# Squares of branch B by whole tiles, key norm rows loaded a head ahead, index scores paced by the heads of C and B

## The chip, the cores and the metric

The kernel runs on one core of one Trainium2 chip. The metric is device time in microseconds (us) of one execution, lower is better. The core has five engines with queues of their own: PE (matmuls; PEld is its weight load), DVE (VectorE), ACT (ScalarE), POOL (GpSimd, used here almost only to issue DMAs) and SP (issues DMAs). Each runs its own instructions in order and waits for others by semaphores.

## The reference

One decoder layer over 512 tokens of width 2048, in float32. `h = rms_norm(x)` is projected once, and the columns feed three branches, a SiLU gate for each, and three merge gates:

```python
# A: sparse attention: index scores pick the 128 best keys of each query
dots  = einsum('bthd,bsd->bths', q_idx, k_idx)           # 16 index heads of 64
score = einsum('bths,bth->bts', relu(dots), w_idx) * IDX_SCALE
_, sel = top_k(where(causal, score, -inf), topk)         # then GQA over sel, 8 heads, bias by distance
# B: latent attention, 8 heads; 192 = 128 plain + 64 rotary
qb = rms_norm((rms_norm(bcq)  @ w_b_uq ).reshape(bsz, seq, 8, 192))
kv =          (rms_norm(bckv) @ w_b_ukv).reshape(bsz, seq, 8, 256)     # 128 key + 128 value
kb = rms_norm(concat([kv[..., :128], k_pe]))             # rotary part shared by the heads
o_b = causal_softmax(rope(qb) @ rope(kb) * 192**-0.5) @ kv[..., 128:]
# C: cross-attention into 256 memory tokens, 4 heads of 256
u = stack([o_a * silu(az), o_b * silu(bz), o_c * silu(cz)])
merged = sum_n sigmoid(gates[n]) * (u[n] @ w_branch[n])
out = x + merged @ w_out
```

The norms of B's queries and keys need, for each token and head, a sum of squares over 128 plain columns, and over 64 rotary columns.

## The kernel before

**Main stream and threads.** `stream` on PE walks a list of weight chunks; each is cut into jobs of 256 weight rows, and a plain job has 24 matmuls of 512 columns. Weights arrive by SP (`wraw`, 512 KB), ACT rounds them to `whi`, DVE subtracts to get the rest `wlo`, and three matmuls (high by high, high by low, low by high) stand for one in float32. Jobs are prepared three ahead (`LOOK = 3`). The order of chunks is: memory keys and values, projections, merge gates (by Strassen products), a z chunk (SiLU gate) of C, `uq0` to `uq2` (B's queries from the latent; `uq2` holds the rotary parts), `ukv0` to `ukv3` (B's keys and values), the other z chunks, then four `w_branch` chunks each for C, B and A (the operand `u` is branch output times gate), and `w_out`. Results collect in PSUM: `pg` and `pn` for the main stream, `pm` for everything else.

All attention work is written as generators ("threads"): `c_thread` and `c_part` (C), `b_thread` and three `b_part` (B; one prepares head after head, the parts do logits, softmax and values for query tiles 0 and 1, 2, 3), `idx_thread` (index scores for eight pairs of heads into `mask1` to `mask3`, then top-k on DVE by 16 rounds of MAX and MATCH_REPLACE a tile), `a_bias_thread` and `a_thread` (A's bias and heads, after B has closed), `u_thread` (loads branch output and gate into `stage`, multiplies, splits into `u`).

**What sets the order.** The program is written once, by a planner: it books a modelled cost for each instruction on its engine, and after each group of three matmuls of the main stream it steps those threads whose inputs the model shows as ready. A `yield` of a list waits in the model for these tiles or for a free `pm` bank; a `yield` of a string waits for a flag set by another thread. These waits only decide where an instruction stands in its engine's queue; on the chip, semaphores for data and buffers are all that is left of them. `defer` puts a piece of work behind one of the next groups of matmuls.

**What the change touches.** `to_dram` evacuates a chunk of B two token tiles at a time into `stage` (one half by ACT, one by DVE), issues the store, and defers the squares: for `uq0`, `uq1` and `ukv*` one ACT square of 128x128 for each head and token tile into `junk` with an accumulated sum in `b_ss`; for `uq2` one whole square of `stage` into another `stage`, then one DVE sum into `r_ss`. `b_thread` makes the norms `rs_b` from `b_ss` and `r_ss`, stores those of the keys as rows in DRAM (`sp_rows`), and for each head loads the four rows broadcast over all partitions as `b_rk` (one buffer): after the three parts of the head before have set the flags `B0 scaled`, `B1 scaled` and `B2 scaled` in `softmax`. `rotate` turns the rotary query part `b_rp` with three scratch tiles `ro_a`, `ro_b`, `ro_c`. The pool `lpool` of the latents (`lraw`, `cqT`, `ckT`) is closed when the second z chunk of C begins on PE; `bpool` opens after that.

Of the kernel before, what the change touches and what calls it, by code (L numbers as in the profile page):

```python
# [10 lines left out]
F32 = mybir.dt.float32  # L11
# [4 lines left out]
OP = mybir.AluOpType  # L16
# [274 lines left out]
class Kern:  # L291
# [638 lines left out]
    def to_dram(self, key, nb, cols, scale=None, sums=(), groups=None):  # L930


        nc = self.nc
        dt = self.spill_tile(key, nb, cols)
        box = {}

        def evac(b, p):
            if b % 2 == 0:
                box["st"] = self.stage()
            st = box["st"]  # L940
            src, dst = p[:, :cols], st[:, b % 2, :cols]
# [12 lines left out]
            def squares():  # L954
                for c0, c1, d in sums:
                    junk = self.wp.tile([P, 512], BF, name="junk", tag="junk")
                    nc.scalar.activation(junk[:, :c1 - c0], st[:, b % 2, c0:c1], AF.Square, accum_out=d(b))
                if b == nb - 1:
                    self.flags.add(key + " sums")
            if sums:  # L960
                self.defer(squares, b == nb - 1)
            if groups and b % 2:
                sq = []

                def whole():
                    sq.append(self.stage())
                    nc.scalar.activation(sq[0], st, AF.Square)

                def total():
                    nc.vector.tensor_reduce(groups[:, b - 1:b + 1], sq[0].rearrange("p t (h c) -> p t h c", h=groups.shape[2]),  # L970
                                            axis=AX.X, op=OP.add)
                    if b == nb - 1:
                        self.flags.add(key + " sums")
                self.defer(whole, False, 2)
                self.defer(total, b == nb - 1)
        return evac
# [72 lines left out]
        tt(dst[:, :, 32:], a, b, op=OP.add)  # L1049


    def softmax(self, pool, blocks, scale, tag, act, bank, masks=None, flag=None):


        nc = self.nc
        n = len(blocks)
        st = pool.tile([P, 4, n], F32, name=tag + "st", tag=tag + "st", bufs=2)
        if masks:
            for i, ((pr, ps), (mk, rk)) in enumerate(zip(blocks, masks)):
                nc.vector.tensor_tensor(pr, ps, rk, op=OP.mult)  # L1060
                nc.vector.tensor_tensor_reduce(pr, pr, mk, 1.0, -3.4e38, OP.add, OP.max, st[:, 0, i:i + 1])
            self.pm.release(bank)
            self.flags.add(flag)
            nc.vector.scalar_tensor_tensor(st[:, 1], st[:, 0], -1.0, scale, op0=OP.mult, op1=OP.mult)
        else:
            for i, (_, ps) in enumerate(blocks):
                nc.vector.tensor_reduce(st[:, 0, i:i + 1], ps, axis=AX.X, op=OP.max, negate=True)
            nc.vector.tensor_tensor(st[:, 1], st[:, 0], scale, op=OP.mult)
        yield [st]
        for i, (pr, ps) in enumerate(blocks):  # L1070
            nc.scalar.activation(pr, pr if masks else ps, AF.Exp, bias=st[:, 1, i:i + 1], scale=scale[:, i:i + 1],
                                 accum_out=st[:, 2, i:i + 1])
        if not masks:
            self.pm.release(bank)
        yield [st]
        nc.vector.reciprocal(st[:, 3], st[:, 2])
        for i, (pr, _) in enumerate(blocks):
            if act:
                if not i:
                    yield [st]  # L1080
                nc.scalar.activation(pr, pr, AF.Copy, scale=st[:, 3, i:i + 1])
            else:
                nc.vector.tensor_scalar(pr, pr, st[:, 3, i:i + 1], None, op0=OP.mult)
# [130 lines left out]
    def b_thread(self):  # L1214
# [5 lines left out]
        with self.slots("bpool", side="right") as pool:  # L1220
# [13 lines left out]
                return rp  # L1234

            def load_scale(h):
                rk = pool.tile([P, T], F32, name="b_rk", tag="b_rk")
                row = rows[8 * h + 4:8 * h + 8]
                nc.gpsimd.dma_start(rk, bass.AP(tensor=row.tensor, offset=row.offset, ap=[[0, P], [1, T]]))
                return rk  # L1240
# [7 lines left out]
            def rotate(rp):  # L1248

                x = rp.rearrange("p t (a d) -> p t a d", a=2)  # L1250
                x1, x2 = x[:, :, :, :32], x[:, :, :, 32:]
                a, b, c = [pool.tile([P, NT, 2, 32], F32, name="ro_" + y, tag="ro_" + y) for y in "abc"]
                sin, cos = [bc(y, [P, NT, 2, 32], 2) for y in (self.sin, self.cos)]
                gain = self.g_bqr.unsqueeze(1).unsqueeze(1).to_broadcast([P, NT, 2, 64])
                tt = nc.vector.tensor_tensor
# [30 lines left out]
            pt = ring.bank([P, 512])  # L1286
            nc.tensor.transpose(pt[:64, :P], rs_b.rearrange("p a b -> p (a b)"), self.ident)
            yield [pt]
            stage = pool.tile([P, T], F32, name="b_rk", tag="b_rk")
            nc.scalar.activation(stage[:64, :P], pt[:64, :P], AF.Copy)  # L1290
            nc.gpsimd.dma_start(rows, stage[:64, :P])
            ring.release(pt)
# [11 lines left out]
            for h in range(8):  # L1304
# [21 lines left out]
                if h % 2 == 0:  # L1326
# [8 lines left out]
                    ring.release(pt)  # L1335
                    if h < 6:
                        rp = load_rope(h + 2)
                if h:
                    for x in range(3):
                        yield "B%d scaled %d" % (x, h - 1)  # L1340
                    rk = load_scale(h)
                self.b_now = (pool, rs, qh, ql, kh, kl, qs[h % 2], rh, rl, rk)
                self.flags.add("b%d" % h)
                if h:
                    yield "B2 %d" % (h - 1)
                vh = pool.tile([P, NT, P], F32R, name="b_vh", tag="b_vh")
                vl = pool.tile([P, NT, P], F32R, name="b_vl", tag="b_vl")
                yield from self.split_in_turn(vh, vl, kv[:, :, P:])
# [11 lines left out]
    def b_part(self, x):  # L1360
# [6 lines left out]
        for h in range(8):  # L1367
# [10 lines left out]
            for t in tiles:  # L1378
# [3 lines left out]
                for i, (a, b) in enumerate(((qh, kh), (qh, kl), (ql, kh), (qs, rh), (qs, rl))):  # L1382
# [3 lines left out]
            self.flags.add("B%d logits %d" % (x, h))  # L1386
            yield [pg, rk]
            yield from self.softmax(pool, blocks, rs[:, tiles[0]:tiles[-1] + 1], "b%d_" % x, True, pg,
                                    [(self.mwide[:, T - (t + 1) * P:], rk[:, :(t + 1) * P]) for t in tiles],
                                    "B%d scaled %d" % (x, h))  # L1390
            yield [pr, ring]
            pt = ring.bank([P, n, P])
            for b in range(n):
# [40 lines left out]
    def idx_thread(self, apre, kpool):  # L1434
# [4 lines left out]
        with self.slots("ipool", line=512) as pool:  # L1439
# [42 lines left out]
                        nc.vector.scalar_tensor_tensor(sc[t], x, iw[:, t, h:h + 1], sc[t], op0=OP.mult, op1=OP.add)  # L1482

            for hp in range(8):
                yield [q]
                s0 = pool.tile([P, 512], F32R, name="i_s0", tag="i_s0")
                s1 = pool.tile([P, 512], F32R, name="i_s1", tag="i_s1")
# [745 lines left out]
    def build(self):  # L2233
# [42 lines left out]
        def close_gates():  # L2276
# [7 lines left out]
            self.ckT = [self.lp.tile([P, 2, T], F32R, name="ckT%d" % i) for i in range(2)]  # L2284
            self.flags.add("gates")

        def close_h():
            yield "z end"
            yield "B closed"
            hpool2.close()  # L2290
            self.bp = bpool.enter_context(self.slots("bp", side="right"))
            self.flags.add("bp")
# [30 lines left out]
        def one(x, b):  # L2323
            return x[:, b:b + 1]
# [36 lines left out]
        pre(close_gates)  # L2361
        wu = A["w_uq"]
        for c in range(3):
            sums = [(j * P, j * P + P, lambda b, h=4 * c + j: one(self.b_ss[:, h], b)) for j in range(4 if c < 2 else 0)]
            self.chunk(wu[:, c * 512:(c + 1) * 512], 4, 512,
                       lambda k: (self.cqT[0][:, k], self.cqT[1][:, k]), "tm", 4,
                       self.to_dram("uq%d" % c, 4, 512, sums=sums, groups=None if sums else self.r_ss), "bcqT")
        wk = A["w_b_ukv"][0]
        for c in range(4):
            sums = [(j * 256, j * 256 + P, lambda b, h=2 * c + j: one(self.b_ss[:, h], 4 + b)) for j in range(2)]  # L2370
            self.chunk(wk[:, c * 512:(c + 1) * 512], 2, 512,
                       lambda k: (self.ckT[0][:, k], self.ckT[1][:, k]), "tm", 4,
                       self.to_dram("ukv%d" % c, 4, 512, sums=sums), "bckvT")
        for key in "ABC":
            for c in range(2):
                self.spill_tile("o%s%d" % (key, c), 4, 512)
        for n, c in ((2, 1), (0, 0), (0, 1), (1, 0), (1, 1)):
            z_chunk(n, c)
            if n == 2:
                self.chunks[-1]["start"] = "kpe"  # L2380
                pre(lambda: (lpool.close(), self.flags.add("latents done")))
        self.chunks[-1]["post"] = lambda: self.flags.add("z end")
        for i in range(2):
            self.spill_tile("m%d" % i, NT, D)
# [7 lines left out]
        def mem_load(eng, a, b):  # L2392
# [4 lines left out]
        w = None  # L2397
        self.first_loads = [w, m(0, 2), m(2, 4), w, m(4, 6), w, m(6, 8), w, m(8, 10), w, m(10, 12), w, m(12, 16), w]
        self.run(self.stream, [
            self.mem_thread(sp, memh, meml), self.x_loads(), self.x_thread(sp), self.mem_stats(sp), self.rotary_tables(), self.latent_thread(), self.u_thread(), self.kpe_thread(), self.c_thread(), self.c_part(0), self.c_part(1), self.b_part(0), self.b_part(1), self.b_part(2), self.b_thread(), self.a_thread(0), self.a_thread(1), self.a_bias_thread(apre, kpool), self.idx_thread(apre, kpool), self.h_ops_thread(), self.t_thread(), close_h()])  # L2400
        tpool.close()
        bpool.close()
        hpool.close()
# [35 lines left out]
```

## Time and profile before

| | |
|---|---|
| median of 3 runs | 1823.47 us (1823.46 to 1825.14) |
| profiled execution: its own time, its span | 1823.97 us, 1822.2 us |
| busy PE, PEld, DVE, ACT, POOL | 1810.0, 1512.8, 1371.7, 972.5, 193.5 us |
| DVE and ACT, 960 to 1040 us (chunks `uq`, `ukv` and around) | 48.0 and 63.3 us of 80 |
| DVE, 1160 to 1320 us (B's heads, top-k) | 148.0 us of 160 |
| top-k rounds on DVE | 1163.7 to 1339.8 us |
| first and last DVE operation on `b_pr` (B's logits) | 1088.9, 1297.6 us |
| last store of A's output (`sp_oA`) | issued at 1553.9 us |

The page's share of busy PE is no measure of waiting, since a matmul's record runs from its start until its result is out, and records overlap: here they start 0.227 us apart and last 0.39 us. What PE lost is seen where two starts stand further apart than the first of them takes in the stream.

### The profile page before, as it was taken

How to read it: one execution, taken by the hardware profiler on the slowest of the kernel's cores; microseconds unless marked ns; L12 is line 12 of the kernel's file. 1: busy time of each engine (PE TensorE's matmuls, PEld its weight loads, DVE VectorE, ACT ScalarE, POOL GpSimd, SP SyncE). 2: the span in 40 equal slices, each digit the busy share in tenths (PEclk: the TensorE clock that was granted, in tenths of full speed). 3: DMA queues.
4: the chain of work that ended last, by engine and by line, in shares of the span. 5: the costliest groups of instructions: out<-in, count | busy, mean ns of one | idle time of the engine just before them, and what ended most of it. 6: DMA issues, size and time to landing. Idle time of an engine off the chain costs nothing.

```text
span 1822.2 us, 24643 instructions
## 1 busy us (share of the span) xinstructions
PE 1810.0 (99%) x9009; PEld 1512.8 (83%) x9009; DVE 1371.7 (75%) x2098; ACT 972.5 (53%) x1740; POOL 193.5 (11%) x286
## 2 busy tenths in 40 slices
PE   9999999999999999999999999999999999899999
PEld 7888888888888888888888888888888888688887
DVE  6888787787777777778775677899986777566755
ACT  7644544554444444444458756545477875244442
POOL 0000101001010100000112121311011111110000
PEclk9999999999999999999999999999999999999999
DMA  9846597787676966756645544444664754746784
GB/s 379 293 161 196 188 331 199 199 215 201 186 291 217 264 189 193 208 162 200 208 158 204 190 152 137 139 155 116 213 238 158 248 162 163 277 162 197 269 268 144
DMA packets 155994, 374.84 MB, mean 206 GB/s; under 512 B 18656, under 2 KB 24192, under 8 KB 154848
## 3 DMA queue, kind: packets, MB, share of 16 engines
q1 hardware_dynamic: 116752, 236.79, 40.8%
q0 software_dynamic: 38976, 136.34, 23.3%
q8 instruction: 71, 1.16, 0.3%
q14 instruction: 51, 0.42, 0.1%
q10 hardware_dynamic: 144, 0.13, 0.0%
HBM read 314.69 MB, written 92.08 MB: 223 GB/s over the span
## 4 chain that ended last, share of the span: by engine, by line
PE 97%; DVE 1%; DMA 1%; ACT 0%; issue 0%; SPq 0%; DVEq 0%
PE pg L157 60%; PE pn L157 27%; PE pm L157 9%; DMA wraw<-w_in 1%; DMA wraw<-w_mem 0%; DVE wlo L157 0%; ACT a_st L157 0%; DVE yg L157 0%; DVE stage L157 0%; SPq L157 0%; DVE T L157 0%; ACT whi L157 0%; DVE bm L157 0%; DVE u L157 0%; DVE mask L157 0%
## 5 line engine op out<-in xcount | busy, mean ns | idle before, releaser
L157 DVE TENSOR_TENSOR wlo<-wraw,whi 128x1024 fp32r<-128x1024 f32 (+2 forms) x267 | 321.6, 1206 | 148.6 <-ACT whi L157 147.2
L157 ACT ACTIVATE whi<-wraw 128x1024 fp32r<-128x1024 f32 (+2 forms) x267 | 278.3, 1044 | 287.9 <-PE pg L157 155.5
L157 PE MATMUL pg<-whi,u 128*128 128x512 f32 x640 | 215.6, 398 | 0.5 <-DVE yg L157 0.5
L157 PE MATMUL pg<-hh,whi 128*128 128x512 f32 x448 | 179.9, 401 | 0.0
L157 PE MATMUL pg<-hh,wlo 128*128 128x512 f32 x448 | 175.3, 391 | 0.0
L157 PE MATMUL pg<-hl,whi 128*128 128x512 f32 x448 | 174.9, 390 | 0.0
L157 ACT ACTIVATE whi<-sraw 128x1024 fp32r<-128x1024 f32 (+1 forms) x99 | 103.7, 1049 | 127.2 <-DVE sraw L157 54.2
L157 DVE TENSOR_TENSOR wlo<-sraw,whi 128x1024 fp32r<-128x1024 f32 (+1 forms) x99 | 119.9, 1213 | 52.1 <-ACT whi L157 51.2
L157 PE MATMUL pg<-whi,hS 128*128 128x512 f32 (+1 forms) x480 | 156.8, 388 | 0.0
L157 PE MATMUL pn<-whi,hS 128*128 128x512 f32 (+1 forms) x480 | 156.1, 386 | 0.0
L157 PEld LDWEIGHTS pg<-whi,u 128*128 128x128 f32 x640 | 120.2, 188 | 23.9 <-DVE yg L157 0.9
L157 PE MATMUL pg<-wlo,u 128*128 128x512 f32 x320 | 124.8, 390 | 0.0
L157 PE MATMUL pg<-wlo,hh 128*128 128x512 f32 (+1 forms) x320 | 123.9, 387 | 0.0
L157 PE MATMUL pn<-wlo,hh 128*128 128x512 f32 (+1 forms) x320 | 123.8, 387 | 0.0
L157 PE MATMUL pg<-whi,hl 128*128 128x512 f32 (+1 forms) x320 | 123.8, 387 | 0.0
L157 PE MATMUL pn<-whi,hl 128*128 128x512 f32 (+1 forms) x320 | 123.8, 387 | 0.0
L157 PE MATMUL pn<-whi,hh 128*128 128x512 f32 (+1 forms) x320 | 123.8, 387 | 0.0
L157 PE MATMUL pg<-whi,hh 128*128 128x512 f32 (+1 forms) x320 | 123.8, 387 | 0.0
L157 ACT ACTIVATE whi<-T 128x1024 fp32r<-128x1024 f32 (+1 forms) x80 | 83.9, 1049 | 68.7 <-PE pn L157 26.0
L157 DVE TENSOR_TENSOR wlo<-T,whi 128x1024 fp32r<-128x1024 f32 (+1 forms) x80 | 96.7, 1209 | 30.4 <-ACT whi L157 30.2
L157 PEld LDWEIGHTS pg<-whi,hS 128*128 128x128 f32 x480 | 90.1, 188 | 18.0
L157 PEld LDWEIGHTS pn<-whi,hS 128*128 128x128 f32 x480 | 90.1, 188 | 17.3
(459 smaller groups left out, 3977.2 us busy)
## 6 DMA issues: line engine op xcount, KB each, us to landing
wraw<-w_in SPq DMA_DIRECT2D x146, 512.0 KB, 4.2
sraw<-w_in SPq DMA_DIRECT2D x90, 512.0 KB, 4.2
wT<-w_out POOLq DMA_DIRECT2D x24, 1024.0 KB, 20.8
wraw<-w_branch SPq DMA_DIRECT2D x48, 512.0 KB, 4.5
yg<-sp_g POOLq DMA_DIRECT2D x24, 512.0 KB, 6.0
wraw<-wT SPq DMA_DIRECT2D x20, 512.0 KB, 3.9
mraw<-w_mem SPq DMA_DIRECT2D x17, 512.0 KB, 8.4
wT<-wT POOLq DMA_DIRECT2D x8, 1024.0 KB, 13.0
```

What stands on the lines that cost most here:

```text
L157: return f(*a, **k)
```

## The change

1. **Squares.** For all `uq` and `ukv` chunks ACT squares both token tiles in one instruction, into a tile of the shape and the single buffer of `lraw`: 1024 columns a partition for `uq0` and `uq1` (four heads) and `uq2` (eight rotary parts), 512 for `ukv*` (only the key halves of two heads). DVE then sums by heads into `b_ss` or `r_ss`. The 64 small squares go.
2. **Latents.** Since `lraw` now serves the squares, the `uq` chunks wait for the second latent too (`"bckvT"`), and `lpool` is closed by a thread of its own, `close_latents`, after `kpe`, `uq2 sums` and `ukv3 sums`.
3. **Key norm rows.** `b_rk` has two buffers; the load for head h+1 stands after head h-1's last output instead of the load for head h after head h-1's last scaling. The flags `scaled` go.
4. **Rotary scratch.** `rotate` takes one `stage` buffer in place of `ro_a`, `ro_b`, `ro_c`.
5. **Pace.** Before each pair of index heads `idx_thread` waits for a flag: pair 0 for C's head 1, pair 1 for C's head 3, pair 2 for the end of C, pairs 4 to 7 for B's heads 1 to 4.

```diff
@@ to_dram
+                n, w, dst_of = groups
                 def whole():
-                    sq.append(self.stage())
-                    nc.scalar.activation(sq[0], st, AF.Square)
+                    y = self.lp.tile([P, NT, 256], F32, name="lraw", tag="lraw")...[:, :2 * n * w]...(t=2, h=n)
+                    sq.append(y)
+                    nc.scalar.activation(y, st[:, :, :cols]...(h=n)[:, :, :, :w], AF.Square)
                 def total():
-                    nc.vector.tensor_reduce(groups[:, b - 1:b + 1], sq[0]..., axis=AX.X, op=OP.add)
+                    nc.vector.tensor_reduce(dst_of(b - 1), sq[0], axis=AX.X, op=OP.add)
@@ b_thread
-                rk = pool.tile([P, T], F32, name="b_rk", tag="b_rk")
+                rk = pool.tile([P, T], F32, name="b_rk", tag="b_rk", bufs=2)
-                a, b, c = [pool.tile([P, NT, 2, 32], F32, name="ro_" + y, tag="ro_" + y) for y in "abc"]
+                room = self.stage().rearrange("p t c -> p (t c)")
+                a, b, c = [room[:, 256 * i:256 * i + 256]... for i in range(3)]
-                if h:
-                    for x in range(3):
-                        yield "B%d scaled %d" % (x, h - 1)
-                    rk = load_scale(h)
                 self.flags.add("b%d" % h)
                 if h:
                     yield "B2 %d" % (h - 1)
+                if h < 7:
+                    rk = load_scale(h + 1)
@@ idx_thread
             for hp in range(8):
+                pace = {0: "c1", 1: "c3", 2: "C"}.get(hp) or hp > 3 and "b%d" % (hp - 3)
+                if pace:
+                    yield pace
@@ build
+        def close_latents():
+            for x in ("kpe", "uq2 sums", "ukv3 sums"):
+                yield x
+            lpool.close()
+            self.flags.add("latents done")
-                       self.to_dram("uq%d" % c, 4, 512, sums=sums, groups=None if sums else self.r_ss), "bcqT")
+                       self.to_dram("uq%d" % c, 4, 512, groups=groups), "bckvT")
-                       self.to_dram("ukv%d" % c, 4, 512, sums=sums), "bckvT")
+                       self.to_dram("ukv%d" % c, 4, 512, groups=groups), "bckvT")
-                pre(lambda: (lpool.close(), self.flags.add("latents done")))
```

PE executes the same 9009 matmuls in both programs, by kind and count. Since the planner writes the order anew, what stands between the first z chunk of C and the start of branch A is in another order.

On ACT, at the evacuation of `uq0`, `junk,b_ss<-stage` is the four small squares of one token tile; its neighbours are index scores (`i_r`, `i_s`) and C's heads (`c_...`). Before:

```order
L157 ACTIVATE stage<-pg 128x512
L157 ACTIVATE junk,b_ss<-stage 128x128 x4
L157 ACTIVATE i_r<-pm_7809 128x512
L157 ACTIVATE i_s_7851<-i_q 64x512
L157 ACTIVATE i_s_7852<-i_q 64x512
L157 ACTIVATE whi<-wraw 128x1024
```

Now, at the first pair of token tiles of `uq0`:

```order
L157 ACTIVATE stage<-pg 128x512
L157 ACTIVATE lraw<-stage 128x1024
L157 ACTIVATE c_qh<-pm_7784,cols 128x512
L157 ACTIVATE c_pr<-pm_7789 128x512
L157 ACTIVATE c_pr<-pm_7802 128x512
L157 ACTIVATE i_r<-pm_7815 128x512
L157 ACTIVATE whi<-wraw 128x1024
```

Eight small squares of a pair of token tiles became one, and C's heads stand further ahead against the weights, with fewer index scores between them.

On SP, at the end of the `w_branch` chunks, `sp_oB` and `sp_oA` are the outputs of B and A, `sp_s` their gates; a `w_branch` load is one job of PE (- before, + now):

```order
 L157 DMA stage<-sp_oB_207 128x1024
-L157 DMA wraw<-w_branch 128x2x512 x2
+L157 DMA wraw<-w_branch 128x2x512 x3
 L157 DMA stage<-sp_s_211 128x1024
-L157 DMA wraw<-w_branch 128x2x512 x14
+L157 DMA wraw<-w_branch 128x2x512 x8
 L157 DMA stage<-sp_oA_204 128x1024
 L157 DMA stage<-sp_s_211 128x1024
 L157 DMA stage<-sp_oA_204 128x1024
-L157 DMA wraw<-w_branch 128x2x512
+L157 DMA wraw<-w_branch 128x2x512 x4
```

The first loads of A's output moved ahead by six jobs against the weights: the first stands behind 31 of the 48 `w_branch` loads instead of 37.

On DVE, at the end of branch B, `yg<-yg,pg` evacuates a bank of the last `w_branch` chunks, `yg<-ym,yg` adds the branches, and `stage<-stage` and `u<-stage,u` make the operand of branch A. Before, the first `u` of A stands behind the evacuation of B's last chunk, `a_pl` being the last splits of A's heads:

```order
L157 TENSOR_TENSOR a_pl<-pm_14390,a_ph 128x512
L157 TENSOR_TENSOR wlo<-wraw,whi 128x1024
L157 SCALAR_TENSOR_TENSOR yg<-yg,pg 128x512
L157 TENSOR_TENSOR wlo<-wraw,whi 128x1024
L157 SCALAR_TENSOR_TENSOR yg<-yg,pg 128x512 x3
L157 TENSOR_TENSOR yg<-ym,yg 128x512 x4
L157 SCALAR_TENSOR_TENSOR stage<-stage 128x1024
L157 TENSOR_TENSOR u<-stage,u 128x1024
```

Now it stands behind the evacuation of B's last chunk but one, with `stage<-stage` still ahead of that:

```order
L157 TENSOR_TENSOR a_pl<-pm_14079,a_ph 128x512
L157 TENSOR_TENSOR yg<-ym,yg 128x512
L157 TENSOR_TENSOR wlo<-wraw,whi 128x1024 x2
L157 SCALAR_TENSOR_TENSOR stage<-stage 128x1024
L157 SCALAR_TENSOR_TENSOR yg<-yg,pg 128x512
L157 TENSOR_TENSOR wlo<-wraw,whi 128x1024
L157 SCALAR_TENSOR_TENSOR yg<-yg,pg 128x512 x3
L157 TENSOR_TENSOR yg<-ym,yg 128x512 x2
L157 TENSOR_TENSOR wlo<-wraw,whi 128x1024
L157 TENSOR_TENSOR yg<-ym,yg 128x512 x2
L157 TENSOR_TENSOR u<-stage,u 128x1024
```

The operand of branch A moved ahead of the four evacuations of B's last chunk. On PE, 42 matmuls of branch B stand between the last matmul of A's heads and the first of branch A before the change, and 171 with it.

More of the change, by code (lines that the diff above doesn't have):

```diff
@@ L963, in evac @@
                 sq = []
+                n, w, dst_of = groups
                 def whole():
-                    sq.append(self.stage())
-                    nc.scalar.activation(sq[0], st, AF.Square)
+                    y = self.lp.tile([P, NT, 256], F32, name="lraw", tag="lraw").rearrange("p t c -> p (t c)")[:, :2 * n * w].rearrange("p (t h c) -> p t h c", t=2, h=n)
+                    sq.append(y)
+                    nc.scalar.activation(y, st[:, :, :cols].rearrange("p t (h c) -> p t h c", h=n)[:, :, :, :w], AF.Square)
                 def total():
-                    nc.vector.tensor_reduce(groups[:, b - 1:b + 1], sq[0].rearrange("p t (h c) -> p t h c", h=groups.shape[2]),
-                                            axis=AX.X, op=OP.add)
+                    nc.vector.tensor_reduce(dst_of(b - 1), sq[0], axis=AX.X, op=OP.add)
                     if b == nb - 1:
@@ L1049, in rotate, with softmax @@
         tt(dst[:, :, 32:], a, b, op=OP.add)
-    def softmax(self, pool, blocks, scale, tag, act, bank, masks=None, flag=None):
+    def softmax(self, pool, blocks, scale, tag, act, bank, masks=None):
         nc = self.nc
@@ L1062, in softmax @@
             self.pm.release(bank)
-            self.flags.add(flag)
             nc.vector.scalar_tensor_tensor(st[:, 1], st[:, 0], -1.0, scale, op0=OP.mult, op1=OP.mult)
@@ L1251, in rotate @@
                 x1, x2 = x[:, :, :, :32], x[:, :, :, 32:]
-                a, b, c = [pool.tile([P, NT, 2, 32], F32, name="ro_" + y, tag="ro_" + y) for y in "abc"]
+                room = self.stage().rearrange("p t c -> p (t c)")
+                a, b, c = [room[:, 256 * i:256 * i + 256].rearrange("p (t a d) -> p t a d", t=NT, a=2) for i in range(3)]
                 sin, cos = [bc(y, [P, NT, 2, 32], 2) for y in (self.sin, self.cos)]
@@ L1288, in b_thread @@
             yield [pt]
-            stage = pool.tile([P, T], F32, name="b_rk", tag="b_rk")
+            stage = pool.tile([P, T], F32, name="b_rk", tag="b_rk", bufs=2)
             nc.scalar.activation(stage[:64, :P], pt[:64, :P], AF.Copy)
@@ L1388, in b_part @@
             yield from self.softmax(pool, blocks, rs[:, tiles[0]:tiles[-1] + 1], "b%d_" % x, True, pg,
-                                    [(self.mwide[:, T - (t + 1) * P:], rk[:, :(t + 1) * P]) for t in tiles],
-                                    "B%d scaled %d" % (x, h))
+                                    [(self.mwide[:, T - (t + 1) * P:], rk[:, :(t + 1) * P]) for t in tiles])
             yield [pr, ring]
@@ L2363, in build @@
         for c in range(3):
-            sums = [(j * P, j * P + P, lambda b, h=4 * c + j: one(self.b_ss[:, h], b)) for j in range(4 if c < 2 else 0)]
+            groups = (4, P, lambda b, c=c: self.b_ss[:, 4 * c:4 * c + 4, b:b + 2].rearrange("p h t -> p t h"))
+            if c == 2:
+                groups = (8, 64, lambda b: self.r_ss[:, b:b + 2])
             self.chunk(wu[:, c * 512:(c + 1) * 512], 4, 512,
                        lambda k: (self.cqT[0][:, k], self.cqT[1][:, k]), "tm", 4,
-                       self.to_dram("uq%d" % c, 4, 512, sums=sums, groups=None if sums else self.r_ss), "bcqT")
+                       self.to_dram("uq%d" % c, 4, 512, groups=groups), "bckvT")
         wk = A["w_b_ukv"][0]
         for c in range(4):
-            sums = [(j * 256, j * 256 + P, lambda b, h=2 * c + j: one(self.b_ss[:, h], 4 + b)) for j in range(2)]
+            groups = (2, P, lambda b, c=c: self.b_ss[:, 2 * c:2 * c + 2, 4 + b:6 + b].rearrange("p h t -> p t h"))
             self.chunk(wk[:, c * 512:(c + 1) * 512], 2, 512,
                        lambda k: (self.ckT[0][:, k], self.ckT[1][:, k]), "tm", 4,
-                       self.to_dram("ukv%d" % c, 4, 512, sums=sums), "bckvT")
+                       self.to_dram("ukv%d" % c, 4, 512, groups=groups), "bckvT")
         for key in "ABC":
@@ L2399, in build @@
         self.run(self.stream, [
-            self.mem_thread(sp, memh, meml), self.x_loads(), self.x_thread(sp), self.mem_stats(sp), self.rotary_tables(), self.latent_thread(), self.u_thread(), self.kpe_thread(), self.c_thread(), self.c_part(0), self.c_part(1), self.b_part(0), self.b_part(1), self.b_part(2), self.b_thread(), self.a_thread(0), self.a_thread(1), self.a_bias_thread(apre, kpool), self.idx_thread(apre, kpool), self.h_ops_thread(), self.t_thread(), close_h()])
+            self.mem_thread(sp, memh, meml), self.x_loads(), self.x_thread(sp), self.mem_stats(sp), self.rotary_tables(), self.latent_thread(), self.u_thread(), self.kpe_thread(), self.c_thread(), self.c_part(0), self.c_part(1), self.b_part(0), self.b_part(1), self.b_part(2), self.b_thread(), self.a_thread(0), self.a_thread(1), self.a_bias_thread(apre, kpool), self.idx_thread(apre, kpool), self.h_ops_thread(), self.t_thread(), close_h(), close_latents()])
         tpool.close()
```

## The prediction

> **What bounds the kernel now.** I read the page's head, then what PE waited for, then the chain of work that ended last and PE's instructions in order of time at the longest of these waits.
>
> ```profile
> span 1822.2 us, 24643 instructions
> PE 1810.0 (99%) x9009; PEld 1512.8 (83%) x9009; DVE 1371.7 (75%) x2098; ACT 972.5 (53%) x1740; POOL 193.5 (11%) x286
> ```
>
> ```profile
> PE pn L157 <- ACT u L157: 5.4, 1, 5.4
> PE pa L157 <- DVE identb L157: 1.5, 1, 1.5
> PE pg L157 <- DVE yg L157: 0.5, 1, 0.5
> PE pg L157 <- ACT whi L157: 0.3, 1, 0.3
> PE pg L157 <- DVE wlo L157: 0.2, 1, 0.2
> ```
>
> The second fence lists all of PE's waits: engine, tile, releaser; total, times, longest in us. Only the first and third lie where the change can reach (1.5 is the start of the program). So the kernel is the stream of matmuls, and other engines count only where they make PE wait. The longest wait in order of time (start, duration, engine, operation, count):
>
> ```profile
> 1561.88 0.39 PE L157 MATMUL pg<-whi,u 128*128 128x512 f32 x1
> 1567.68 0.80 PE L157 MATMUL pn<-whi,u 128*128 128x512 f32 x1 [5.41 <-ACT u L157]
> 1568.27 0.63 PE L157 MATMUL pn<-wlo,u 128*128 128x512 f32 x1
> 1568.94 1.22 PE L157 MATMUL pn<-whi,u 128*128 128x512 f32 x2
> 1569.96 0.63 PE L157 MATMUL pn<-wlo,u 128*128 128x512 f32 x1
> 1570.38 1.05 PE L157 MATMUL pn<-whi,u 128*128 128x512 f32 x2
> 1571.24 0.63 PE L157 MATMUL pn<-wlo,u 128*128 128x512 f32 x1
> 1571.66 1.05 PE L157 MATMUL pn<-whi,u 128*128 128x512 f32 x2
> 1572.52 0.63 PE L157 MATMUL pn<-wlo,u 128*128 128x512 f32 x1
> 1572.94 0.84 PE L157 MATMUL pn<-whi,u 128*128 128x512 f32 x2
> 1573.62 0.39 PE L157 MATMUL pn<-wlo,u 128*128 128x512 f32 x1
> ```
>
> The chain of work around it, merged (start, us, what), and two stages by windows (after the window and its length: busy time and count of PE, PEld, DVE, ACT, POOL, then granted clock, DMA share, GB/s):
>
> ```profile
> 1552.07 0.68 PE pm L157 x3
> 1552.75 9.53 PE pg L157 x42
> ...
> 1562.91 2.49 DVE yg L157 x4
> 1565.40 1.15 DVE stage L157
> ...
> 1566.57 1.07 ACT u L157
> ...
> 1592.94 5.44 PE pg L157 x24
> ```
>
> ```profile
> 1560.00:1600.00 40.00, 34.55 (x141) 27.12 (x140) 25.23 (x30) 11.07 (x12) 7.14 (x10) 0.91 0.73 257
> 1720.00:1760.00 40.00, 40.00 (x179) 33.10 (x177) 25.58 (x28) 17.01 (x17) 1.41 (x2) 1.00 0.86 289
> ```
>
> A matmul of 512 columns takes 5.44 / 24 = 0.227 us of the stream. The first matmul of branch A starts 1567.68 - 1561.88 = 5.80 us after the last of branch B, so 5.57 us are lost. Then the 13 matmuls from 1567.68 to 1573.62 take 5.94 us instead of 13 x 0.227 = 2.95: another 2.99 us, with starts 0.43 us apart, and the window's granted clock is 0.91 against 1.00. The place costs **8.56 us**. The chain says why: A's heads end at 1552.75 on PE, only 42 matmuls of cover follow, and the operand `u` is made by evacuations (`yg`), `stage` and `u` one after the other.
>
> The Trainium skill, page "TensorE: Matmul & The Clock Gate", Part 1, has the array at half clock after an idle window of about 3.4 us until about 3.4 us of sustained work. The trace agrees in kind; by that rule the pace would cost 1.7 us and the place 7.3, by the rows it is 2.99 and 8.56, and I take the rows.
>
> **The change part by part.** PE's matmuls are the same 9009, so nothing is added to or taken from the stream itself; each part is worth what it does to the waits.
>
> *Squares.* Small squares on ACT (start, duration), the nearest rows for whole ones on ACT and sums on DVE (count | busy, mean ns of one), and the stage of the `uq` and `ukv` chunks by windows:
>
> ```profile
> 977.38 0.31 ACT L157 ACTIVATE junk<-stage 128x128 bf16<-128x128 f32 x1
> 977.82 0.31 ACT L157 ACTIVATE junk<-stage 128x128 bf16<-128x128 f32 x1
> ```
>
> ```profile
> L157 ACT ACTIVATE whi<-wraw 128x1024 fp32r<-128x1024 f32 x250 | 264.2, 1058 | 273.9 <-PE pg L157 152.3 <-PE pn L157 68.9 <-DVE wraw L157 46.3
> L157 ACT ACTIVATE u<-u 128x512 f32<-128x512 f32 x24 | 15.2, 633 | 26.7 <-DVE u L157 26.2
> L157 DVE TENSOR_REDUCE r_ss<-stage 128x16 f32<-128x1024 f32 x2 | 2.4, 1215 | 0.1
> ```
>
> ```profile
> 972.00:1020.00 48.00, 48.00 (x225) 40.13 (x224) 25.84 (x31) 42.62 (x150) 8.03 (x15) 1.00 0.71 240
> ```
>
> A small square with its accumulator read occupies ACT for 977.82 - 977.38 = 0.44 us. There are 64 (two chunks of four heads and four of two, four token tiles each): 28.2 us go. In their place come 4 x 1.06 + 8 x 0.63 = 9.3 us (the two squares of `uq2` stay): ACT gains 18.9 us. DVE takes on 4 sums of 1024 at 1.215 and 8 of 512, between half of that and all of it: 9.7 to 14.6 us, 9.7 taken, since 512 columns are half the elements. In the 48 us of this stage ACT was busy for 42.6 and DVE for 25.8; it becomes about 24 and 36 before the other moves. Both hide behind PE's 48, so the part's own price is 0. What it does is open ACT where C's heads and the scores queued behind the squares.
>
> *One buffer of `lraw`, and `uq` behind the second latent.* A square waits for the sum before it, and `whi` stands behind it on ACT; weights are made three jobs ahead, 3 x 5.44 = 16.3 us, against 1.2 us for a sum and what is ahead of it. The second latent's last transposes stand 56 matmuls of 512 columns (12.7 us) and more ahead of `uq0` on PE. 0 for both.
>
> *Key norm rows.* What the issue of `b_rk` on POOL waited for before (us, times), and its DMA:
>
> ```profile
> L157 POOL DMA_DIRECT2D b_rk<-sp_rows x8: 549/552/579, 1073.1 to 1275.7; - x8
> ...
>   DVE b_pr L157: 10.4, 3
> ```
>
> Eight loads before and now, 0.55 us of POOL each; issued a head earlier, they no longer hold POOL for `b_pr`, with the loads of q and kv queued behind. PE waited for none of it: 0 directly, and B's heads follow each other closer.
>
> *Rotary scratch.* Same seven DVE operations, but three of them work in one of the four `stage` buffers, which the evacuations share; four times in the program, while a z chunk needs two every eight jobs. 0.
>
> *Pace.* These waits exist when the program is written; nothing queues behind them on an engine. The scores are moved, not reduced. DVE where scores, B's heads and top-k met:
>
> ```profile
> 1160.00:1200.00 40.00, 40.00 (x202) 33.79 (x201) 36.07 (x108) 15.77 (x29) 15.16 (x29) 1.00 0.52 151
> 1280.00:1320.00 40.00, 40.00 (x194) 33.66 (x194) 38.53 (x74) 17.75 (x32) 0.55 (x1) 1.00 0.59 204
> ```
>
> DVE is at 90 to 96% there. C's and B's heads now come first and the scores last: in the written order A's first matmul stands 412 matmuls nearer to the start, A's last 129.
>
> *What that does to the wait.* From A's last matmuls (1552.07) to the first of branch A (1567.68) the way by store, load, `stage` and `u` takes 15.6 us. Before, 42 matmuls cover it, 9.5 us; now 171, 38.8 us: 23 to spare. On DVE the first `u` now stands behind the evacuations of B's last chunk but one; after such evacuations 2.49 + 1.15 + 1.07 us and one more split of 1.2 are left, against a last chunk of 96 x 0.227 = 21.8 us, of which the first 5.4 pass before the buffer of `u` is free. So the 5.57 go, and with them the slow pace: -8.56. Next to be late there is the third `u`, behind the last chunk's evacuations, but it is wanted two jobs, 10.9 us, later.
>
> *The 0.5 us wait.* At a bank that DVE had not evacuated:
>
> ```profile
> 1347.96 0.39 PE L157 MATMUL pg<-whi,u 128*128 128x512 f32 x1
> 1348.81 0.50 PE L157 MATMUL pg<-whi,u 128*128 128x512 f32 x1 [0.47 <-DVE yg L157]
> ```
>
> It costs 0.85 - 0.23 = 0.62. DVE's work there is dealt anew: between 0.62 less and as much more; I take 0.3 less, nearer to its going, since B closes earlier.
>
> **Sum.** 8.56 + 0.3 = 8.9 us off the profiled execution's own 1823.97: 1815.1. The median of the runs is 0.5 lower, so the forecast is **1814.6 us** (-0.49%).
>
> **Rivals.**
> - *The mask becomes the last thing.* Top-k of the third tile now ends 16 weight tiles (`wlo`) of DVE's queue ahead of A's last split, against 27 before. If scores at the back hold A's heads up, PE meets a wait at A's logits instead of at `u`. For it: DVE at 96%. Against it: the order already holds A's later place with 23 us to spare. A wait of 5.6 us there would be priced like the old one, back to 1823.5; a wait of 2 us, with no slow pace, gives 1816.6. It decides when it passes 5 us.
> - *Slower: the one `lraw` buffer.* Each of 14 squares on ACT waits for the sum before it, whose place on DVE is behind C's heads. If 1.2 us of each were met by PE, 14 x 1.2 = 16.8 us: 1831.4. It needs more than 0.64 us for each (8.9 / 14) to end above before, and 12.6 us in all to pass 0.2%. Against it: DVE's 36 of 48 us, and the 16.3 us of weights made ahead.
> - *It does nothing at the place that counts.* The last loads of A's output still come late, since DMA landing, not the order, held `u`: 1823.5 stays. Against it: six jobs, 32.6 us, of move on SP.
>
> **How the numbers follow.** About 0.2% (3.6 us) is what a measurement of this kernel can tell from no change. The forecast gets 0.80; the mask 0.12, of it 0.03 with a wait short enough to end below 1819.8; slower 0.04; no effect 0.04. Faster: 0.80 + 0.03 = 0.83; within 0.2%: 0.09 + 0.03 = 0.12 (one part in four of "no effect" goes to worse order elsewhere); slower 0.05. Low end: both waits gone whole and 0.7 for other order, 1823.5 - 9.2 - 0.7 = 1813.6. High end: a new wait of about 3.4 us with 2.5 of slow pace, 1814.6 + 5.9 = 1820.5, which leaves out most of the mask's case, no effect, and slower.
>
> **What would show it.** Right: PE's list of waits without the row of `u`; the windows around the start of branch A at 40.0 us of PE and clock 1.00; span near 1813.3; ACT's busy time some 19 us less and its small squares gone, DVE's some 10 more, in a stage where ACT has room; the last store of A's output some 29 us further ahead of branch A's first matmul. Wrong: a new row among PE's waits, at `pm` (A's logits, a late mask), at `whi` or `pg` between 970 and 1020 (the `lraw` buffer), or at `u` still, each with a slow stretch behind it when it is as long as the old one.

## The result and the profile after

The changed kernel takes 1814.35 us (median of 6 runs, 1813.94 to 1815.14) against 1823.7 us (6 runs): 9.35 us less, ratio 0.9948 (95% interval 0.9935 to 0.9961). The profiled execution took 1815.14 us. The forecast was 1814.6 us with a range of 1813.6 to 1820.5.

The page's head after, and all that PE waited for (engine, tile, releaser; total, times, longest in us):

```profile
span 1813.4 us, 24535 instructions
PE 1806.4 (100%) x9009; PEld 1511.5 (83%) x9009; DVE 1378.1 (76%) x2110; ACT 958.0 (53%) x1624; POOL 193.2 (11%) x286
```

```profile
PE pa L157 <- DVE identb L157: 1.5, 1, 1.5
PE pg L157 <- ACT whi L157: 0.6, 1, 0.6
PE pn L157 <- DVE wlo L157: 0.4, 1, 0.4
PE pg L157 <- DVE wlo L157: 0.2, 1, 0.2
```

The rows of `u` (5.4 us) and of `yg` (0.5) are gone and nothing has come in between 900 us and the end; what is left lies before 400 us, ahead of what the change touches. Summed over all starts of matmuls from 900 us on that stand over 0.12 us further apart than the plain pace, PE lost 9.33 us before and 0.13 now: these 9.20 us are nearly the whole 9.35 of the medians. PE's instructions at the start of branch A (`pg` is B's last bank, `pn` A's first), and the windows of the two stages that the prediction spoke of:

```profile
1561.97 0.39 PE L157 MATMUL pg<-whi,u 128*128 128x512 f32 x1
1562.20 0.39 PE L157 MATMUL pn<-whi,u 128*128 128x512 f32 x1
```

```profile
972.00:1020.00 48.00, 48.00 (x263) 41.30 (x262) 35.69 (x61) 31.51 (x57) 10.49 (x17) 1.00 0.62 207
1560.00:1600.00 40.00, 40.00 (x186) 33.14 (x185) 23.98 (x31) 12.93 (x17) 7.12 (x10) 1.00 0.76 264
```

Branch A follows B after 0.23 us, the plain pace, and the second window has a granted clock of 1.00 where it had 0.91. DVE there shows why: the first `u` is done at 1549.35, 12.8 us before it is used, ahead of the evacuations of B's last chunk (`yg<-yg,pg`). A bracket at the end of a row gives how long the engine stood idle just before it, and what ended that:

```profile
1548.12 1.23 DVE L157 TENSOR_TENSOR u<-stage,u 128x1024 fp32r<-128x1024 f32 x1 [2.81 <-ACT u L157]
...
1558.32 0.69 DVE L157 SCALAR_TENSOR_TENSOR yg<-yg,pg 128x512 f32<-128x512 f32 x1 [2.35 <-PE pg L157]
```

The stage of the `uq` and `ukv` chunks by the tile `lraw` (count, duration in ns min/median/max, first and last start; then who waited for the tile, us and times):

```profile
L157 ACT ACTIVATE lraw<-stage x14: 623/634/1064, 968.3 to 1033.1; 128x512 f32<-128x512 f32 x8, 128x1024 f32<-128x1024 f32 x6
L157 DVE TENSOR_REDUCE b_ss<-lraw x12: 678/687/1221, 974.8 to 1034.1; 128x4 f32<-128x512 f32 x8, 128x8 f32<-128x1024 f32 x4
...
  ACT lraw L157: 13.3, 9
```

ACT did wait for sums behind the one buffer, 13.3 us in nine places, and PE met none of it. And the stores of A's output (POOL, first and last issue):

```profile
L157 POOL DMA_DIRECT2D sp_oA<-bm x8: 710/716/748, 1326.8 to 1524.5; - x8
```

The last was issued at 1553.9 us before, so it is 29.4 us earlier. Branch A's first matmul came 5.5 us earlier too, so the store stands 37.7 us ahead of it where it stood 13.8: 23.9 us further, not the 29 that the prediction gave as a sign.

### The profile page after: what moved, and what is told of

It is laid out like the page before. It is cut to its first block, busy times and chain, and to the rows that moved or that the text cites. A ratio compares the mean times of both kernels' runs of the same rounds, so it can differ in the third digit from the quotient of the medians.

```text
span 1813.4 us, 24535 instructions
## 1 busy us (share of the span) xinstructions
PE 1806.4 (100%) x9009; PEld 1511.5 (83%) x9009; DVE 1378.1 (76%) x2110; ACT 958.0 (53%) x1624; POOL 193.2 (11%) x286
## 4 chain that ended last, share of the span: by engine, by line
PE 98%; DMA 1%; DVE 1%; SPq 0%; issue 0%; ACT 0%; DVEq 0%
PE pg L157 61%; PE pn L157 27%; PE pm L157 9%; DMA wraw<-w_in 1%; DMA wraw<-w_mem 0%; DVE wlo L157 0%; SPq L157 0%; DVE T L157 0%; DVE u L157 0%; DVE wraw L157 0%; DVE stage L157 0%; ACT whi L157 0%; PE pb L157 0%; DVE x_r L157 0%; PE pa L157 0%
```

## The experiments

Each kernel is compared with the kernel before, timed beside it (medians 1824.2 to 1824.5 us, against the 1823.7 of the result); so a difference under 1 us between kernels timed apart says nothing. "Cover" is the number of branch B's matmuls that the written order has between the last matmul of A's heads and the first of branch A: 42 before, 171 after. "Lost" is a distance between two matmul starts less the 0.227 us of the plain pace.

The theory at the start was that of cover: the way from A's heads by store, load, `stage` and `u` takes 15.6 us, and what the matmuls do not cover is lost. Its rival: DVE's written order alone decides, by what stands ahead of the first `u`.

### One part at a time

**e1_squares**, parts 1 and 2 alone:

```diff
-                    sq.append(self.stage())
-                    nc.scalar.activation(sq[0], st, AF.Square)
+                    y = self.lp.tile([P, NT, 256], F32, name="lraw", tag="lraw")...
+                    nc.scalar.activation(y, ..., AF.Square)
...
+            groups = (4, P, lambda b, c=c: ...)     # uq; (2, P, ...) for ukv
```

> Before, with the squares by whole tiles and the latents' new order alone (parts 1 and 2). In its written order 120 matmuls of branch B stand between the last matmul of A's heads and the first of branch A (42 before, 171 with the whole change). Cover theory: only this cover counts; 120 x 0.227 = 27.2 us against the 15.6 us that the way from A's heads to the operand took: no wait at u, no slow pace, 1814.5 us (1813.8 to 1816). Rival 'relief' (fewer instructions on ACT in the stage of the squares are the gain): the same 1814.5. Rival 'pace' (moving the index scores is the gain): as before, 1823.7.

Measured: 1814.3 us, ratio 0.9943 (0.9928 to 0.9958), as expected. No wait of PE at `u`; the last store of A's output is issued at 1535.8 us. This part alone brings the whole gain.

**e2_rows**, parts 3 and 4 alone:

```diff
-                rk = pool.tile([P, T], F32, name="b_rk", tag="b_rk")
+                rk = pool.tile([P, T], F32, name="b_rk", tag="b_rk", bufs=2)
...
-                    rk = load_scale(h)
+                if h < 7:
+                    rk = load_scale(h + 1)
```

> Before, with the key norm rows in two buffers and the rotary scratch in a stage buffer alone (parts 3 and 4). In its written order 0 matmuls of cover are left. Cover theory: slower than before; the way of 11 (without the evacuations that stood in it) to 15.6 us is met by PE whole, and 3 us of slow pace follow: 1814.4 + 14 to 18.6 = 1828 to 1833. Rivals 'relief' and 'pace': as before, 1823.7.

Measured: 1835.42 us, ratio 1.0058 (1.0043 to 1.0073), slower as forecast, and 2.4 us past the end of the range. A's heads end right ahead of branch A, with no cover. The chain at branch A's start, by the timelines of POOL, SP and DVE of this kernel:

```profile
1562.91 0.71 POOL L157 DMA_DIRECT2D sp_m<-yg  x1 [22.44 <-DVE yg L157]
1564.38 0.72 POOL L157 DMA_DIRECT2D sp_m<-yg  x1 [0.76 <-DVE yg L157]
1565.10 1.48 POOL L157 DMA_DIRECT2D sp_oA<-bm  x2
```

```profile
1569.10 0.34 SPq L157 DMA_DIRECT2D stage<-sp_oA  x1
```

```profile
1577.53 1.23 DVE L157 SCALAR_TENSOR_TENSOR stage<-stage 128x1024 f32<-128x1024 f32 x1 [13.72 <-DMA stage<-sp_oA]
```

DVE stands 13.72 us for the DMA, and PE loses 18.05 us, then 3.16 by the slow pace. This is the way that the theory of cover spoke of, longer than its 15.6 us.

**e3_pace**, part 5 alone:

```diff
             for hp in range(8):
+                pace = {0: "c1", 1: "c3", 2: "C"}.get(hp) or hp > 3 and "b%d" % (hp - 3)
+                if pace:
+                    yield pace
```

> Before, with the pace of the index scores alone (part 5). 51 matmuls of cover: 11.6 us. Cover theory: a wait of 15.6 - 11.6 = 4.0 us at u, 0 to 5; with it 3 us of slow pace if the wait is past some 3 us: 1818.4 to 1821.5, between the two kernels. Rival 'pace': all of the gain, 1814.4. Rival 'relief': none, 1823.7.

Measured: 1823.93 us, ratio 0.9998 (0.9988 to 1.0008), a miss. The cover grew from 42 to 51 matmuls, the last store came 2.9 us earlier (1551.0), and PE still lost the 5.57 us:

```profile
PE pn L157 <- ACT u L157: 5.4, 1, 5.4
```

By the theory of cover 9 more matmuls are worth 2 us. They were worth nothing, although the load of A's first output was issued 7.3 us earlier, too (at 1546.35 us instead of 1553.61).

**e4_rows_pace** has the edits of e2_rows and e3_pace together, **e8_squares_rows** those of e1_squares and e2_rows, **e12_squares_pace** those of e1_squares and e3_pace:

```diff
+                rk = pool.tile([P, T], F32, name="b_rk", tag="b_rk", bufs=2)     # e4, e8
+                    yield pace                                                   # e4, e12
+                    nc.scalar.activation(y, ..., AF.Square)                      # e8, e12
```

> The change without the squares and the latents (parts 3, 4 and 5). 75 matmuls of cover: 17.0 us, 1.4 more than the way of 15.6. Cover theory: no wait, or one under 2 us without slow pace: 1814.4 to 1816.5. Rival 'relief': no gain, 1823.7. Rival 'pace': all of it, as the cover theory has it too.

> The change without the pace of the index scores (parts 1 to 4). 75 matmuls of cover: 17.0 us. Cover theory: no wait, or one under 2 us: 1814.4 to 1816.5. Rival 'pace': no gain, 1823.7.

> Parts 1, 2 and 5 without the key norm rows and the rotary scratch. 138 matmuls of cover. Theory of order and theory of cover both: no wait at u, 1814.3 us as with the squares alone (1814.3) and the whole change (1814.35). A rival, that the rows in two buffers carry a share of the gain: 1815 us or more.

Measured: e4_rows_pace 1817.48 us, 0.9961 (0.9947 to 0.9976); e8_squares_rows 1821.08 us, 0.9982 (0.9972 to 0.9991); e12_squares_pace 1813.89 us, 0.9944 (0.9927 to 0.996). The first and the second lie above the 1814.4 to 1816.5 that the theory of cover gave; e12 came as expected. In e4 and e8 the first `u` is in time and later ones are not. PE's waits in e4 and in e8:

```profile
PE pn L157 <- DVE u L157: 2.0, 2, 1.5
```

```profile
PE pn L157 <- DVE u L157: 1.7, 1, 1.7
PE pn L157 <- ACT u L157: 1.3, 1, 1.3
PE pg L157 <- DVE stage L157: 0.9, 1, 0.9
```

The last of these rows lies elsewhere, among B's heads: 1.09 us lost at 1219 us, where a bank was evacuated late.

The parts do not add: squares alone gain about 10 us, rows alone lose 11, pace alone is worth nothing, yet pace added to the rows gains 18 (1835.42 to 1817.48), and rows added to the squares lose 7. What they have in common is that each moves where A's heads end. What the last store's issue in each kernel (from the trace) and PE's loss at the start of branch A say together:

| kernel | last store of A's output, us | lost early in branch A, us | time, us |
|---|---|---|---|
| after | 1524.5 | 0 | 1814.35 |
| e12_squares_pace | 1531.9 | 0 | 1813.89 |
| e1_squares | 1535.8 | 0 | 1814.3 |
| e4_rows_pace | 1545.3 | 1.70 + 0.59 | 1817.48 |
| e8_squares_rows | 1547.4 | 1.45 + 1.82 | 1821.08 |
| e3_pace | 1551.0 | 5.57 + slow pace | 1823.93 |
| before | 1553.9 | 5.57 + slow pace | 1823.7 |
| e2_rows | 1565.7 | 18.05 + slow pace | 1835.42 |

Time goes by the end of A's heads, but not by a slope: nothing is lost for an end up to 1536, and the same 5.57 at 1551.0 and at 1553.9. A way that has to be covered would have made these last two differ by 2 to 3 us.

### The load alone made late

The whole change, with A's first output load held until branch B's first (e5), second (e6) or third (e7) operand was used up; cover and A's heads as in the changed kernel:

```diff
                     for x in (("C",), ("B closed",), ("A",))[2 - n]:
                         yield x
+                    if n == 0:
+                        yield "u1 out 0"          # e6: "u1 out 1", e7: "u1 out 2"
```

> The whole change, but the first load of A's output held back in the written order until the second job of branch B's last chunk: three jobs, 16.3 us, are left to PE. Before, 14.1 us passed from the issue of this load to branch A's first matmul. Cover theory: no wait, 1814.4 us (to 1815.5). Nothing else differs, so a rival by which the place where A's heads end counts for itself has 1814.4 too.

> As before, but held back until the third job: 10.9 us left. Cover theory: a wait of up to 14.1 - 10.9 = 3.2 us, likelier 1 to 2, since no evacuations stand between; no slow pace behind it: 1815.4 to 1817.6. Rival (the place where A's heads end counts, not when the load is made): 1814.4.

> As before, but held back until the fourth job, 5.4 us left. Cover theory: a wait of 5.5 to 8.7 us, and 3 us of slow pace behind it: 1822.9 to 1826.1, the time of before again. Rival (slow pace does not come from the wait): 1819.9 to 1823.1, with starts 0.227 us apart behind the wait. Rival (place of A's heads counts): 1814.4.

Measured: e5_late_16 1815.13 us, 0.995 (0.9935 to 0.9965); e6_late_11 1823.61 us, 0.9997 (0.9988 to 1.0006); e7_late_5 1823.82 us, 0.9998 (0.9989 to 1.0008). The e5 kernel came as expected. The e6 kernel missed its 1815.4 to 1817.6, and e7 fell into its range, though not by the length of the way: the first load of e6 was issued at 1548.08 us and that of e7 at 1554.20, 6 us apart, and both lost 5.57 us, as the kernel before did. DVE in e6:

```profile
1551.80 1.23 DVE L157 TENSOR_TENSOR wlo<-wraw,whi 128x1024 fp32r<-128x1024 f32 x1 [4.21 <-ACT whi L157]
1557.51 0.69 DVE L157 SCALAR_TENSOR_TENSOR yg<-yg,pg 128x512 f32<-128x512 f32 x1 [4.48 <-PE pg L157]
...
1561.59 0.69 DVE L157 SCALAR_TENSOR_TENSOR yg<-yg,pg 128x512 f32<-128x512 f32 x1 [0.67 <-PE pg L157]
1562.19 2.49 DVE L157 TENSOR_TENSOR yg<-ym,yg 128x512 f32<-128x512 f32 x4
1564.60 1.22 DVE L157 SCALAR_TENSOR_TENSOR stage<-stage 128x1024 f32<-128x1024 f32 x1
```

and the same place in the kernel before:

```profile
1565.32 1.22 DVE L157 SCALAR_TENSOR_TENSOR stage<-stage 128x1024 f32<-128x1024 f32 x1
```

Neither `stage` row ends in a bracket: DVE did not wait for its data there. In e6 the load was there 7.2 us after its issue, at 1555.3, while DVE stood idle until 1557.51, and `u` was still not made. DVE came to `stage` when the four evacuations of B's last chunk and four adds were done, and the last evacuation waits for PE's last matmul of B. From there an evacuation, four adds, `stage`, and then ACT's half of `u` follow one another until PE starts: 1561.59 to 1566.96 us, 5.4, the wait that the profile gives. Where the first `u` is written ahead of these evacuations, as in e5 (load issued at 1543.26), the wait is 0. The kernel e8 shows the same with a late load. It was issued at 1551.24, later than in e3 and e6, but `stage` stands ahead of the evacuations and starts as soon as the load is there, and branch A's first matmul follows B's last at the plain pace:

```profile
1559.57 1.23 DVE L157 SCALAR_TENSOR_TENSOR stage<-stage 128x1024 f32<-128x1024 f32 x1 [4.66 <-DMA stage<-sp_oA]
```

So it is the place in DVE's queue that sets the 5.57 us of the kernel before, of e3, e6 and e7. In the kernel before the load was not early either. Its issue on SP and the time to its landing:

```profile
L157 SPq DMA_DIRECT2D stage<-sp_oA x1: 339/339/339, 1553.6 to 1553.6; - x1
...
DMA to landing us min/median/max: 8.3/8.3/8.3
```

It was there at 1561.9, 3.4 us before `stage` started. From `stage` to PE it takes another 2.36 us (1565.32 to 1567.68), and without a wait PE would have gone on at 1562.1. An estimate from these numbers: with nothing ahead of `stage` in the queue PE would still have lost some 2.2 us of the 5.57 to the load.

### What stands ahead of `u` moved away

The kernel before, with the four adds of B's last chunk and their store written behind A's second operand (e9); the same on e6 (e10) and on e2 (e11; its expectation says behind the first operand, but in its trace, too, the adds follow the second, at 1578.09 us). Of the four adds one follows the second operand directly, the others stand behind the next weight split:

```diff
+            if i == 2 and c == 0 and k == 2:
+                self.later, self.hold = self.later + self.hold, []
...
+            if i == 1 and c == 3:
+                self.hold = getattr(self, "hold", []) + [rest]
+                return
             self.defer(rest, b == 3, 1)
```

> The kernel before, with one thing changed: DVE's four adds of the last chunk of branch B (yg<-ym,yg, 2.49 us in a row) and their store stand behind the first two operands u of branch A instead of ahead of the first. The same 42 matmuls of cover, the same place of A's stores and loads. Theory of order (u waits for what stands ahead of it on DVE, its data have long landed): PE's wait at branch A's first matmul shrinks by 2.5 us, from 5.57 to 3.1 us lost. If the slow pace of 3.0 us follows a gap of 3.1 us: 1823.7 - 2.5 = 1821.2 us; if it needs a longer gap: 1818.2 us. Theory of late data (the way by store and load is what the cover must hide): the loss stays 5.57 us and the time 1823.7 us.

> The whole change with A's first load held back by two jobs as in e6_late_11 (1823.61 us, 5.57 us lost, 171 matmuls of cover), and the four adds of branch B's last chunk moved behind the first two operands u as in e9_adds_later. Theory of order: 3.1 us lost, 1821.1 us with the slow pace, 1818.1 without. Theory of late data: the load is as late as in e6_late_11, so 5.57 us and 1823.6 us stay.

> Parts 3 and 4 alone as in e2_rows (1835.42 us, 18.05 us lost at branch A's first matmul, no cover), with the four adds of branch B's last chunk moved behind the first operand u. Here the data land last (13.72 us of DMA wait at stage), so both theories say that the adds do not matter: 18 us lost and 1835.4 us within 1 us. If the theory of order held without limit, 2.5 us would go: 1832.9 us.

Measured: e9_adds_later 1824.59 us, 1.0003 (0.9993 to 1.0013); e10_late_adds_later 1824.63 us, 1.0002 (0.9993 to 1.0012). The times miss, and for the wait the theory of order hits. PE and DVE in e9:

```profile
1561.96 0.39 PE L157 MATMUL pg<-whi,u 128*128 128x512 f32 x1
1565.41 0.79 PE L157 MATMUL pn<-whi,u 128*128 128x512 f32 x1 [3.06 <-ACT u L157]
...
1579.43 0.39 PE L157 MATMUL pn<-whi,u 128*128 128x512 f32 x1
1581.95 0.64 PE L157 MATMUL pn<-whi,u 128*128 128x512 f32 x1 [2.14 <-ACT u L157]
```

```profile
1563.04 1.23 DVE L157 SCALAR_TENSOR_TENSOR stage<-stage 128x1024 f32<-128x1024 f32 x1
...
1576.65 1.89 DVE L157 TENSOR_TENSOR yg<-ym,yg 128x512 f32<-128x512 f32 x3
1578.46 1.22 DVE L157 SCALAR_TENSOR_TENSOR stage<-stage 128x1024 f32<-128x1024 f32 x1
```

PE's first loss shrank from 5.57 to 3.22 us (3.16 in e10), by 2.35 of the 2.49 that the adds take; the theory of late data said that it would stay. In e10 the load had been there since 1556.1 (issued at 1548.50, 7.6 us), so the 3.16 left there are order again. In e9 order had no more to give: the load, issued at 1553.69, took 9.3 us and was there at 1563.0, just as `stage` started. And the adds now stand ahead of the third operand's `stage`, and PE lost 2.30 us there, in e9 as in e10. The work that was pushed back came due some 14 us later, and both gaps were followed by slow pace.

**e11_rows_adds_later**: 1828.0 us, ratio 1.002 (1.0011 to 1.003), 7.4 us less than e2_rows, where both theories expected nothing; PE's first loss is 10.53 us instead of 18.05. Its rows for the three that stand above for e2, from POOL, SP and DVE:

```profile
1562.75 1.46 POOL L157 DMA_DIRECT2D sp_oA<-bm  x2 [22.29 <-ACT bm L157]
```

```profile
1565.56 0.34 SPq L157 DMA_DIRECT2D stage<-sp_oA  x1
```

```profile
1569.99 1.23 DVE L157 SCALAR_TENSOR_TENSOR stage<-stage 128x1024 f32<-128x1024 f32 x1 [8.61 <-DMA stage<-sp_oA]
```

`stage` starts 7.54 us earlier (1577.53 to 1569.99): 2.35 because POOL no longer issues B's two stores ahead of A's last two, 1.19 more up to the load's issue, and 4.00 because the load is there 4.43 us after its issue instead of 8.43. In e2 POOL went on from its stores to the loads of branch A's gates and sums; in e11 neither B's stores nor these loads had been issued by then. So the way by store and load, where it does decide, was made longer by B's own last transfers: 2.35 us of it are seen in POOL's order. That the other 5.19 come from the traffic is inferred, not shown by a run of its own.

## Why the prediction was right

**The place and its price.** Right: 8.56 us of 5.57 and 2.99 were forecast to go, and both went. With the 0.62 at 1348 us they are 9.18, against the 9.20 that PE's starts show gone.

**The 0.5 us wait.** Taken as 0.3 less; all of the 0.62 went. This is the term that was mis-sized, and 0.3 us of the sum.

**The way of 15.6 us and its cover.** The forecast held for another reason than this step gave. The 15.6 us contained the time that `stage` stood behind B's evacuations on DVE, so it was no length that matmuls have to cover: e6 and e7 have 171 matmuls after A's heads and lose what 42 lost, and e3's nine more bought nothing. Real lateness exists (18.05 us in e2, 10.53 in e11); in the kernel before it was second, with an estimated 2.2 of the 5.57 us. What carried the forecast was the step beside it, the order on DVE: the first `u` ahead of the evacuations of B's last chunk. In so far as the cover was the ground for the number, that is luck. The earlier end of A's heads seems to act by way of the order, in that it lets the planner write `u` there: e5 to e7 show that it goes behind the evacuations when the load alone is held back. At which point the planner changes over is left open.

**Squares.** Right that they hide: PE is at 48.0 of 48. ACT gained 14.5 us (972.5 to 958.0), not 18.9, and DVE took on 6.4, not 9.7. The new squares cost the 9.3 that were forecast, so the 64 small ones had been worth 23.8 us of busy time, an estimated 0.37 each, and not the 0.44 between two starts. A sum of 512 columns took 687 ns, against 608 taken. The window's ACT came to 31.5 of "about 24", because C's operations moved into the room, which is what the part was said to do. Its DVE came to 35.7 of "about 36" by luck: the sums take 8.7 us there and took 2.4 before, and C's operations brought most of the rest. That this part alone brings the gain (e1) was not said.

**Key norm rows: 0.** Right within the whole change (without these rows, e12, it takes 1813.89), wrong as a price of the part: alone it costs 11 us (e2). A's heads then end 11.8 us later (last store 1553.9 to 1565.7); what holds them up in the stages between is left open.

**Pace: 0.** Right alone (e3) and beside the squares (e12); beside the rows it is worth 18 us (e2 to e4).

**The rivals.** The mask as the last thing did not come: the list of PE's waits has no row at `pm`. The one `lraw` buffer made ACT wait 13.3 us, against the 16.8 priced, but PE met none of it. No effect: it had the landing and not the order hold `u`. In the kernel before the order came last, 3.4 us after the landing. The move on SP came, but by e6 it would not have sufficed had `u` stayed behind the evacuations.

## What to carry to other kernels

Where an engine waits for an operand, read first what ran on the producing engine just ahead of it and whether that instruction has a bracket: without one its data were there, and the queue's order decides. Then read how long they had been there, from the load's issue and its time to landing: 9.3 us in e6, 3.4 in the kernel before, next to nothing in e9. That is what a better order can win at most. A part that frees an engine early can decide what is written ahead of what hundreds of us later, so parts of a change to such a planned order are to be tried alone and together: here they were worth -10, +11 and 0, and -9.4 in one. Work pushed behind a late operand comes due at the next one, so a shorter wait is only a gain once the rows behind it have been read too.

## What the runs showed of the hardware

**The slow pace follows shorter gaps than expected.** In e9 the first gap lost 3.22 us and the second 2.30. Windows of the stretches behind each gap, and of the one between and the one after (granted clock in the third column from the end):

```profile
1565.40:1571.90 6.50, 6.46 (x14) 4.63 (x15) 5.31 (x5) 1.06 (x1) 0.00 (x0) 0.50 0.77 243
1572.00:1579.40 7.40, 7.40 (x34) 6.14 (x33) 3.90 (x5) 1.06 (x1) 1.29 (x2) 1.00 0.52 193
1581.90:1585.50 3.60, 3.35 (x7) 2.16 (x8) 3.57 (x4) 1.06 (x2) 2.85 (x4) 0.54 0.64 211
1586.00:1590.00 4.00, 4.00 (x19) 3.32 (x18) 0.64 (x1) 0.34 (x1) 0.00 (x0) 1.00 0.88 287
```

A gap of 2.30 us was followed by half clock, here and in e10, while in the profile of e8 gaps of 1.45 and 1.82 left it at 1.00 behind them. In e10 the clock still stood at 1.00 until 1582.0 us, 1.9 us after PE had started again behind the second gap. These are single profiles, and e8's other executions show mean clocks from 1.000 down to 0.998, with times from 1818.44 to 1822.78 us, so no sharp border is shown. The Trainium skill, page "TensorE: Matmul & The Clock Gate", Part 1, gives about 3.4 us of idling for this; the trace does not agree, and the measurement decides. Nor does what the slow stretch costs grow with the gap: 2.99 us after 5.57, 3.16 after 18.05, 3.36 after 3.22 and 1.95 after 3.16 (e10). It goes by how much of the half clock is left when PE starts again. By windows the granted clock is 0.50 from 1566.6 to 1573.4 us in the kernel before (PE starts again at 1567.68), from 1565.6 to 1585.9 in e2 (at 1579.90) and from 1565.1 to 1568.4 in e10 (at 1564.96). Half of what is left, an estimate of the cost, is 2.9, 3.0 and 1.7 us. The same section has the window run freely, so that the number of slow matmuls differs from run to run; those costs fit that.

**The same load lands sooner or later.** The first load of A's output, 512 KB, was there 4.43 us after its issue in e11, 5.0 in e3, 8.43 in e2 and 9.3 in e9. While it was awaited, the share of busy DMA engines (the second column from the end) was 0.91 in e2 and 0.80 in e11:

```profile
1569.10:1577.50 8.40, 0.00 (x0) 0.00 (x0) 0.00 (x0) 0.00 (x0) 1.20 (x2) 0.50 0.91 297
1565.56:1569.99 4.43, 0.00 (x0) 0.00 (x0) 0.00 (x1) 0.00 (x0) 0.00 (x0) 0.61 0.80 219
```

The difference fits the other transfers that e2 had in flight; no run varies them alone.
